# FFN pair products: t2 made by a third accumulating transfer, the splits in another order, and product 1 with 512 columns

## Chip, core and metric

The kernel runs on one core of a Trainium2 chip, with 512 tokens, in fp32. The time is device microseconds of one execution. A core has a matrix engine (PE, with its weight loads as PEld), a vector engine (DVE), an activation engine (ACT), GpSimd (POOL) and a queue engine that mostly issues transfers (SP, "sync"). Each engine runs its own instructions in order.

## The reference, cut to what matters

One layer of a hybrid encoder: a SwiGLU feed-forward half step (FFN1), a token mixer of two attention branches with gates, and a second feed-forward half step (FFN2). The model width is 1024 and D_FF is 2816.

```python
def _swiglu(x, w_gate, w_up, w_down):
    return (jax.nn.silu(x @ w_gate) * (x @ w_up)) @ w_down
...
        f = _swiglu(_rmsnorm(x, ffn1_pre_g[l]), ffn1_w_gate[l], ffn1_w_up[l], ffn1_w_down[l])
        x = x + 0.5 * _rmsnorm(f, ffn1_post_g[l])
...
        f = _swiglu(_rmsnorm(x, ffn2_pre_g[l]), ffn2_w_gate[l], ffn2_w_up[l], ffn2_w_down[l])
        x = x + 0.5 * _rmsnorm(f, ffn2_post_g[l])
```

The change touches the products `x @ w_gate` and `x @ w_up` of both feed-forward steps.

## The kernel before, in words

**Products in parts.** Every fp32 operand is split in a high and a low part (`split`: ACT rounds a copy at L113, DVE subtracts it at L114), and a product is taken in three passes, high by high, high by low and low by high (`mm3`, L204 to L206). The 2816 features of gate and up are 22 blocks of 128. Two blocks of each are done plainly. The other 20 are *pairs* j = 0 to 19: gate block j and up block j are the two rows of a 2 by 2 block product (the other two divisions are the two halves of the 1024 inputs and the two halves, 256 each, of the tokens).

**Seven products.** A 2 by 2 product by the Strassen-Winograd scheme needs seven products of 512 inputs by 128 features by 256 tokens instead of eight, and sums of weight blocks ahead of them. For a pair, with `gate` and `up` as 128 by 1024 blocks whose halves are [:512] and [512:], the weight blocks by the number of their product are

- 1 and 2: gate[:512] and gate[512:], the two halves of one 512 KB tile `raw`, of which a ring holds two
- 3: up[512:], named w11
- 5: t1 = up[:512] + gate[:512], loaded by SP and then summed by an accumulating transfer that POOL issues (L404)
- 7: t3 = up[:512] + up[512:], in the same way (L405)
- 6: t2 = t1 + w11, a DVE addition (L410, in `sums_of`)
- 4: t4 = t2 + gate[512:], a DVE addition (L415)

`load_blocks` issues the transfers of a pair two pairs ahead; `ready(j + 1, i)` prepares (sums and splits) block i of the next pair while PE works on pair j, in the program's order 1, 5, 2, 6, 3, 7, 4. A ring of 38 tiles of 256 KB (`up`) holds the blocks and results, a ring of 12 the split weights (`w`).

**Wide and narrow products.** A narrow product is 12 matmuls of 256 columns. A wide one (`WIDE`, L461 and L464) puts the high and the low part of the tokens side by side: four matmuls of 512 columns, weight-high by [high | low], fill a whole PSUM bank with two halves, and four of 256 columns add weight-low by high to the lower half. The two halves are summed by whoever reads the bank. Before the change product 1 is always narrow; products 5, 6, 3, 7 and 4 are wide in the pairs of `state["wide"]` (4 to 17 in FFN1, all in FFN2), and product 2 up to pair 16. For pairs 0 to 3 products 1 and 2 are made earlier (`EARLY`).

**Order on PE.** In iteration j PE runs 1(j); the 512-column halves of 7(j-1) and 5(j), then their 256-column halves; then the 512-column halves of 2(j), 6(j), 4(j-1) and 3(j), then theirs. This order is pinned to the program's. Bank q holds 1(j), then 6(j), 7(j), 4(j) are added in it; p holds 5(j), then 3(j); r holds 2(j).

**Readers of the banks.** ACT copies q after product 1 into g (L495). DVE subtracts q after 7(j-1) from a copy of p (L506, with L507 adding the halves), adds r to g (L521, two additions for the two halves), and after 6 and 3 makes the up results (L529, L536, L537). DVE and ACT keep the order that the framework's scheduler gives them when the kernel is built; SP is in the program's order in FFN1. There SP's queue also carries up to seven small transfers of the attention bias for each pair (L1247).

Of the kernel before, what the change touches and what calls it, by code (L numbers as in the profile page):

```python
# [16 lines left out]
ALU = mybir.AluOpType  # L17
# [7 lines left out]
NF = 2816 // P  # L25
# [1 line left out]
EPS = 1e-6  # L27
NEG = -1.0e30
NUNIT = 38
WIDE = (5, 2, 6, 3, 7, 4)  # L30
PIECE = 1024
NPIECE = 6
SPREAD = 4
# [2 lines left out]
STD = 2  # L36
EARLY = 4
# [9 lines left out]
def block_kernel(ctx, tc, x, gains, weights, rpb_near, rpb_all, alibi0, alibi12, out):  # L47
    nc = tc.nc
# [12 lines left out]
    def unit(dt=F32, name="u"):  # L61
        return up.tile([P, 512], dt, tag="u", name=name)
# [57 lines left out]
    state = {"used": False, "next": 0, "take": 0, "stop": EARLY + 2 * STD, "ahead": lambda: None}  # L120
# [231 lines left out]
    def combined():  # L352
# [17 lines left out]
        for n, of in ((5, lambda i: (whole[0][i], whole[1][i], sub)), (6, lambda i: (v[5][i], a[0][i], sub)),  # L370
# [5 lines left out]
            for i in range(2):  # L376
                if n in WIDE:
                    t = twin("v").rearrange("p (k s t) -> p k s t", k=2, s=2)
# [7 lines left out]
        whole.clear()  # L386
        yield mv

    def load_blocks(n0, j):

        w11, t1, t3 = unit(name="w11"), unit(name="t1"), unit(name="t3")
        gate, up = (n0 + j, n0 + EARLY + 2 * STD + j) if j < EARLY else [n0 + 2 * STD + 2 * j + i for i in range(2)]
        nc.sync.dma_start(t1, weights[up][:, :512])
        nc.sync.dma_start(t3, weights[up][:, :512])
        raw = {3: w11, 5: t1, 7: t3}
        if j < EARLY:
            raw[4] = unit(name="t4")
            nc.sync.dma_start(raw[4], weights[gate][:, 512:])
        else:
            r = wp.tile([P, PIECE], F32, tag="raw", name="raw", bufs=2)  # L400
            nc.sync.dma_start(r, weights[gate])
            raw[1], raw[2] = r[:, :512], r[:, 512:]
        nc.sync.dma_start(w11, weights[up][:, 512:])
        nc.gpsimd.dma_start(t1, weights[gate][:, :512], accum_op=ALU.add)  # L404
        nc.gpsimd.dma_start(t3, weights[up][:, 512:], accum_op=ALU.add)  # L405
        return raw

    def sums_of(raw):
        raw[6] = unit(name="t2")
        nc.vector.tensor_tensor(raw[6], raw[5], raw[3], op=ALU.add)  # L410
        if 4 in raw:
            nc.vector.tensor_tensor(raw[4], raw[6], raw[4], op=ALU.add)
        else:
            raw[4] = unit(name="t4")
            nc.vector.tensor_tensor(raw[4], raw[6], raw[2], op=ALU.add)  # L415

    def split_block(raw):
        w = wp.tile([P, PIECE], F32R, tag="w", name="w")
        split(w[:, :512], w[:, 512:], raw)
        return w  # L420

    def seven(use, mv, n_pairs, n0, behind, far, lead, raws, early, put, pin):

        blocks = {}
        o = {}

        def get(j):
            if j < n_pairs and j > 2:
                raws[j] = load_blocks(n0, j)
            if j >= n_pairs - 1:
                behind(far)

        def ready(j, i):
            if j < n_pairs:
                if j and loads:
                    loads.popleft()()  # L440
                if i == 1:
                    sums_of(raws[j])
                if j >= EARLY or i not in (1, 2):
                    blocks[j, i] = split_block(raws[j].pop(i))
            else:
                behind(lead)

        def product(j, i, key, start):
            if start:
                o[key, j] = bank(key)  # L450
            w = blocks.pop((j, i))
            high = [w[:, k * P:(k + 1) * P] for k in range(4)]
            low = [w[:, 512 + k * P:512 + (k + 1) * P] for k in range(4)]
            acc = o[key, j][:, :256]
            if i not in WIDE or j not in state["wide"] or (key in "qr" and j < EARLY) or (i == 2 and j > NF - STD - 4):
                for k in range(4):
                    mm3(acc, high[k], low[k], *mv[i][k][:2], start and k == 0, k == 3, skip_group_check=True)
                return
            for k in range(4):
                to = shaped(o[key, j], mv[i][k][2])  # L460
                nc.tensor.matmul(to, high[k], mv[i][k][2], start=start and k == 0, stop=False, skip_group_check=True)  # L461
            yield
            for k in range(4):
                nc.tensor.matmul(acc, low[k], mv[i][k][0], start=False, stop=k == 3, skip_group_check=True)  # L464

        def run(*products):
            products = [product(*p) for p in products]
            for _ in range(2):
                for p in products:
                    next(p, None)  # L470

        def full(j):
            return j in state["wide"] and j >= EARLY

        res = {}
        get(0)
        get(1)
        blocks[0, 5] = split_block(raws[0][5])
        ready(0, 1)
        raws[0].pop(5)  # L480
        for i in (6, 3, 7, 4):
            ready(0, i)
            if i == 3:
                put()
        begin = mark()
        for j in range(n_pairs + 1):
            now, was = j < n_pairs, j > 0
            get(j + 2)
            if now:
                if j < EARLY:  # L490
                    o["q", j], g = early[j]
                else:
                    run((j, 1, "q", True))
                    g = unit(name="g")
                    nc.scalar.copy(g[:, :256], o["q", j][:, :256])  # L495
                u = unit(name="up")
                res[j] = g, u, unit(name="p5") if j in state["wide"] else u[:, 256:]
            ready(j + 1, 1)
            if pin and j == 0:
                pool.append((pin, mark(), (mybir.EngineType.DVE,)))  # L500
            run(*[(j - 1, 7, "q", False)] * was, *[(j, 5, "p", True)] * now)
            if was:
                g0, u0, s0 = res.pop(j - 1)
                q0 = o["q", j - 1]
                if full(j - 1):
                    nc.vector.tensor_tensor(s0, s0, q0, op=ALU.subtract)  # L506
                    nc.vector.tensor_tensor(u0[:, 256:], s0[:, :256], s0[:, 256:], op=ALU.add)  # L507
                else:
                    nc.vector.tensor_tensor(u0[:, 256:], s0[:, :256], q0[:, :256], op=ALU.subtract)
                if j - 1 in state["wide"] and not full(j - 1):  # L510
                    nc.vector.tensor_tensor(u0[:, 256:], u0[:, 256:], s0[:, 256:], op=ALU.add)
            ready(j + 1, 5)
            if now:
                p = o["p", j]
                nc.scalar.copy(res[j][2], p if j in state["wide"] else p[:, :256])
            ready(j + 1, 2)
            two = now and j >= EARLY
            run(*[(j, 2, "r", True)] * two, *[(j, 6, "q", False)] * now, *[(j - 1, 4, "q", False)] * was, *[(j, 3, "p", False)] * now)
            if two:
                for part in range(1 + (full(j) and j <= NF - STD - 4)):  # L520
                    nc.vector.tensor_tensor(g[:, :256], g[:, :256], o["r", j][:, part * 256:part * 256 + 256], op=ALU.add)  # L521
            ready(j + 1, 6)
            if now:
                nc.scalar.copy(u if full(j) else u[:, :256], o["q", j] if full(j) else o["q", j][:, :256])
            ready(j + 1, 3)
            if was:
                if full(j - 1):
                    nc.scalar.copy(g0[:, 256:], q0[:, 256:])
                    nc.vector.tensor_tensor(g0[:, 256:], q0[:, :256], g0[:, 256:], op=ALU.add)  # L529
                    use(j - 1, g0, u0, g0[:, 256:])  # L530
                else:
                    use(j - 1, g0, u0, q0[:, :256])
            ready(j + 1, 7)
            if now:
                if full(j):
                    nc.vector.tensor_tensor(u, p, u, op=ALU.subtract)  # L536
                    nc.vector.tensor_tensor(u[:, :256], u[:, :256], u[:, 256:], op=ALU.add)  # L537
                else:
                    nc.vector.tensor_tensor(u[:, :256], p[:, :256], u[:, :256], op=ALU.subtract)
                if j in state["wide"] and not full(j):  # L540
                    nc.vector.tensor_tensor(u[:, :256], p[:, 256:], u[:, :256], op=ALU.add)
            ready(j + 1, 4)
        pool.append((begin, mark(), (mybir.EngineType.PE,)))
# [1025 lines left out]
    raws = []  # L1569
# [9 lines left out]
    for n in range(2, 4):  # L1579
        raw = wp.tile([P, PIECE], F32, tag="raw", name="raw", bufs=2)  # L1580
# [233 lines left out]
```

## Time and profile before

| | us |
|---|---|
| median of 3 runs (1069.28 to 1071.21) | 1069.45 |
| the profiled execution | 1069.0 |
| its span, first to last instruction | 1067.1 |
| PE busy | 1059.0 |
| DVE busy | 871.7 |
| ACT busy | 650.7 |
| POOL busy | 196.8 |

A row of a timeline is start, duration, engine, line of the kernel, operation, output and inputs, and in brackets the idle time before it and what ended that. Names stand without their buffer numbers there, so a block made in a ring shows as `w` or `t`. "DMA to landing" is the time from the issue of a transfer to its last byte as seen by who waits for it. PE's matmuls overlap, so the distance from start to start tells what one costs, and the duration when its result is there.

### The profile page before, as it was taken

The numbers are of one execution on the slowest core, as the hardware profiler recorded it, in microseconds if no ns is written. First come the engines' busy times: TensorE is split into PE (matmuls) and PEld (weight loads), VectorE is DVE, ScalarE is ACT, GpSimd is POOL, SyncE is SP. The second block draws the span as 40 slices with busy tenths as digits, with TensorE's granted clock in tenths as the row PEclk, the third lists the DMA queues.
The fourth block names the chain that finished last, engine by engine and source line by source line (L and its number), as shares of the span: only waits on it lengthen the run. The fifth ranks groups of instructions, "written<-read, shape, count | busy, mean of one in ns | idle before, by whom it ended". The sixth has DMA issues, their size and how long they took to land.

```text
span 1067.1 us, 17185 instructions
## 1 busy us (share of the span) xinstructions
PE 1059.0 (99%) x5955; PEld 922.5 (86%) x5955; DVE 871.7 (82%) x1694; ACT 650.7 (61%) x1346; POOL 196.8 (18%) x261
## 2 busy tenths in 40 slices
PE   9999999999999999999999999999999999999997
PEld 7899988998888988888988888889899899988886
DVE  7999999989987566676876643877998999989985
ACT  7656656566674665567756641366655566667671
POOL 4112111024334000001100001043301111124201
PEclk9999999999999999999999999999999999999999
DMA  9988988679993554322232239585937777879942
GB/s 335 201 217 234 236 206 202 194 187 264 248 311 115 157 168 150 119 71 69 81 106 79 79 115 304 151 199 191 285 93 191 175 189 198 219 205 246 219 180 80
DMA packets 98026, 193.95 MB, mean 182 GB/s; under 512 B 24337, under 2 KB 26897, under 8 KB 97938
## 3 DMA queue, kind: packets, MB, share of 16 engines
q1 hardware_dynamic: 69760, 138.37, 38.7%
q0 software_dynamic: 25488, 54.01, 27.9%
q8 instruction: 47, 0.77, 0.3%
q10 hardware_dynamic: 2690, 0.46, 0.2%
q14 instruction: 41, 0.34, 0.1%
HBM read 185.68 MB, written 9.68 MB: 183 GB/s over the span
## 4 chain that ended last, share of the span: by engine, by line
PE 99%; DMA 0%; DVE 0%; ACT 0%; SPq 0%; issue 0%; DVEq 0%; ACTq 0%
PE ps L204 11%; PE ps L206 11%; PE ps L205 11%; PE q L461 8%; PE q L206 7%; PE q L205 7%; PE q L204 7%; PE p L461 6%; PE q L464 4%; PE p L464 3%; PE r L461 2%; PE c L206 2%; PE c L205 2%; PE c L204 2%; PE r L205 1%; PE r L206 1%
## 5 line engine op out<-in xcount | busy, mean ns | idle before, releaser
L114 DVE TENSOR_TENSOR w<-raw,w 128x512 fp32r<-128x512 f32 (+1 forms) x142 | 130.8, 925 | 72.5 <-ACT w L113 69.2
L113 ACT CAST w<-t 128x512 fp32r<-128x512 f32 x160 | 98.1, 622 | 113.9 <-DVE t L410 62.9
L113 ACT CAST w<-raw 128x512 fp32r<-128x512 f32 (+1 forms) x142 | 114.0, 809 | 78.8 <-PE ps L205 30.8
L204 PE MATMUL ps<-hn,w 128*128 128x512 f32 (+1 forms) x360 | 136.6, 379 | 0.0
L206 PE MATMUL ps<-hn,w 128*128 128x512 f32 (+1 forms) x360 | 134.6, 374 | 0.0
L205 PE MATMUL ps<-hn,w 128*128 128x512 f32 (+1 forms) x360 | 134.4, 373 | 0.0
L114 DVE TENSOR_TENSOR w<-t,w 128x512 fp32r<-128x512 f32 x160 | 108.2, 684 | 0.2
L404 POOL DMA_DIRECT2D t<-in_weights_dram x40 | 35.0, 875 | 286.5 <-DVE w L114 78.1
L206 PEld LDWEIGHTS ps<-hn,w 128*128 128x128 f32 x360 | 67.8, 188 | 12.7 <-DVE w L114 0.7
L204 PEld LDWEIGHTS ps<-hn,w 128*128 128x128 f32 x360 | 67.9, 189 | 11.4
L205 PEld LDWEIGHTS ps<-hn,w 128*128 128x128 f32 x360 | 67.9, 189 | 10.9
L461 PE MATMUL p<-v,w 128*128 128x512 f32 x272 | 73.1, 390 | 0.0
L113 ACT CAST w<-room 128x1024 fp32r<-128x1024 f32 x49 | 51.5, 1053 | 30.1 <-PE q L206 9.3
L114 DVE TENSOR_TENSOR w<-room,w 128x1024 fp32r<-128x1024 f32 x49 | 59.6, 1220 | 7.1 <-ACT w L113 3.1
L461 PE MATMUL q<-v,w 128*128 128x512 f32 x240 | 65.1, 393 | 0.0
L461 PEld LDWEIGHTS p<-v,w 128*128 128x128 f32 x272 | 50.4, 188 | 10.2
L731 POOL DMA_DIRECT2D rows<-in_weights_dram x36 | 35.3, 1199 | 93.3 <-DVE w L114 62.8
L461 PEld LDWEIGHTS q<-v,w 128*128 128x128 f32 x240 | 43.0, 189 | 7.5
L113 ACT CAST w<-rows 128x512 fp32r<-128x512 f32 x62 | 36.0, 618 | 20.2 <-PE q L206 7.2
L206 PE MATMUL q<-hn,w 128*128 128x256 f32 x168 | 47.6, 283 | 0.0
L205 PE MATMUL q<-hn,w 128*128 128x256 f32 x168 | 47.5, 283 | 0.0
L204 PE MATMUL q<-hn,w 128*128 128x256 f32 x168 | 47.5, 283 | 0.0
(335 smaller groups left out, 3015.0 us busy)
## 6 DMA issues: line engine op xcount, KB each, us to landing
raw<-in_weights_dram SPq DMA_DIRECT2D x94, 512.0 KB
t<-in_weights_dram SPq DMA_DIRECT2D x88, 256.0 KB
t<-in_weights_dram POOLq DMA_DIRECT2D x80, 256.0 KB, 5.9
room<-in_weights_dram SPq DMA_DIRECT2D x37, 512.0 KB
room<-in_weights_dram POOLq DMA_DIRECT2D x29, 512.0 KB, 11.7
w<-in_weights_dram SPq DMA_DIRECT2D x40, 256.0 KB
rows<-in_weights_dram POOLq DMA_DIRECT2D x36, 256.0 KB, 7.8
w<-in_weights_dram POOLq DMA_DIRECT2D x32, 256.0 KB, 8.0
```

The lines of the kernel that those rows point to most:

```text
L113: nc.scalar.copy(hi, src)
L114: nc.vector.tensor_tensor(lo, src, hi.bitcast(F32), op=ALU.subtract)
L204: nc.tensor.matmul(o, sh, mh, start=start, stop=False, **kw)
L205: nc.tensor.matmul(o, sh, ml, start=False, stop=False, **kw)
L206: nc.tensor.matmul(o, sl, mh, start=False, stop=stop, **kw)
L404: nc.gpsimd.dma_start(t1, weights[gate][:, :512], accum_op=ALU.add)
L461: nc.tensor.matmul(to, high[k], mv[i][k][2], start=start and k == 0, stop=False, skip_group_check=True)
L464: nc.tensor.matmul(acc, low[k], mv[i][k][0], start=False, stop=k == 3, skip_group_check=True)
L731: nc.gpsimd.dma_start(u, block(*add, d)[:, cs], accum_op=ALU.add)
```

## The change

Two things are changed, for pairs 4 to 16 of each FFN. *Product 1 becomes wide*: eight matmuls instead of twelve (5955 matmuls become 5851 in the kernel). ACT still copies the lower half of q into g, and a new DVE addition (L511 of the changed kernel) adds the upper half to g; 6(j), which writes into the same bank, has to wait until that has read it. *t2 is no longer summed by DVE*: the blocks are split in the order 5, 1, 2, 3, 6, 7, 4; when t1 has been split (5), POOL issues a third accumulating transfer that adds up[512:] from the memory onto t1's own tile (L458), which makes t2 there; 6 is split from it, and t4 is summed at the end, just before it is split (L454). With that, `raw` is held until the sum of t4. DVE has one addition of 512 columns less and one of 256 columns more in a pair; the memory is read for 256 KB more in a pair.

```diff
-WIDE = (5, 2, 6, 3, 7, 4)
+WIDE = (1, 5, 2, 6, 3, 7, 4)
...
+    def up_block(n0, j):
+        return weights[n0 + 2 * STD + 2 * j + 1]
+
...
-                if i == 1:
-                    sums_of(raws[j])
-                if j >= EARLY or i not in (1, 2):
-                    blocks[j, i] = split_block(raws[j].pop(i))
+                raw = raws[j]
+                if not EARLY <= j <= NF - STD - 4:
+                    if i == 1:
+                        sums_of(raw)
+                    if j >= EARLY or i not in (1, 2):
+                        blocks[j, i] = split_block(raw.pop(i))
+                    return
+                i = {1: 5, 5: 1, 6: 3, 3: 6}.get(i, i)
+                if i == 4:
+                    raw[4] = unit(name="t4")
+                    nc.vector.tensor_tensor(raw[4], raw.pop(6), raw.pop(2), op=ALU.add)
+                blocks[j, i] = split_block(raw[i] if i in (2, 5, 6) else raw.pop(i))
+                if i == 5:
+                    raw[6] = raw.pop(5)
+                    nc.gpsimd.dma_start(raw[6], up_block(n0, j)[:, 512:], accum_op=ALU.add)
...
-            if i not in WIDE or j not in state["wide"] or (key in "qr" and j < EARLY) or (i == 2 and j > NF - STD - 4):
+            if i not in WIDE or j not in state["wide"] or (key in "qr" and j < EARLY) or (i in (1, 2) and j > NF - STD - 4):
...
+                    if full(j) and j <= NF - STD - 4:
+                        nc.vector.tensor_tensor(g[:, :256], g[:, :256], o["q", j][:, 256:], op=ALU.add)
```

The lines behind the first of these stand 3, then 14 to 16 further on in the changed kernel: L404, L405 are L407, L408 there; L506, L507 are L522, L523; L521 is L537; L529, L536, L537 are L545, L552, L553; L461 is L475.

On DVE, in iteration 10 of FFN1, these rows follow the subtraction of q after 7(9) (p5 is the copy of p of pair 9, g the gate result of pair 10, r and q banks). Before, with the sums and splits of blocks of pair 11:

```order
L506 TENSOR_TENSOR p5_1716<-p5_1716,q_1700 128x512
L410 TENSOR_TENSOR t2_1843<-t1_1691,w11_1690 128x512
L507 TENSOR_TENSOR up_1715<-p5_1716 128x256
L415 TENSOR_TENSOR t4_1845<-t2_1843,raw_1695 128x512
L114 TENSOR_TENSOR w_1914<-t2_1843,w_1914 128x512
L114 TENSOR_TENSOR w_1919<-w11_1690,w_1919 128x512
L114 TENSOR_TENSOR w_1929<-t3_1692,w_1929 128x512
L521 TENSOR_TENSOR g_1838<-g_1838,r_1878 128x256 x2
```

After, from the sum of t4 of pair 10 to the splits of t2 and t3 of pair 11:

```order
L454 TENSOR_TENSOR t4_1785<-t1_1551,raw_1555 128x512
L522 TENSOR_TENSOR p5_1692<-p5_1692,q_1679 128x512
L114 TENSOR_TENSOR w_1787<-t4_1785,w_1787 128x512
L523 TENSOR_TENSOR up_1691<-p5_1692 128x256
L114 TENSOR_TENSOR w_1815<-t1_1670,w_1815 128x512
L114 TENSOR_TENSOR w_1839<-raw_1674,w_1839 128x512
L114 TENSOR_TENSOR w_1844<-raw_1674,w_1844 128x512
L114 TENSOR_TENSOR w_1883<-w11_1669,w_1883 128x512
L511 TENSOR_TENSOR g_1809<-g_1809,q_1800 128x256
L114 TENSOR_TENSOR w_1888<-t1_1670,w_1888 128x512
L114 TENSOR_TENSOR w_1898<-t3_1671,w_1898 128x512
```

The subtraction of p5 stands ahead of the splits of t4, t1, both halves of raw and w11, and the new addition of q's upper half to g behind all of them. So it is in pairs 6, 8, 10, 12, 14 and 16 of FFN1; in the others it stands directly ahead of the subtraction.

On DVE in FFN2, around the end of iteration 6 and the beginning of 7 (p5 of pair 6, g of pair 7). Before, from the split of t4 of pair 7 to that of t2 of pair 8:

```order
L114 TENSOR_TENSOR w_9294<-t4_9210,w_9294 128x512
L536 TENSOR_TENSOR up_9206<-p_9219,up_9206 128x512
L114 TENSOR_TENSOR w_9328<-raw_9186,w_9328 128x512
L529 TENSOR_TENSOR g_9086<-q_9073,g_9086 128x256
L537 TENSOR_TENSOR up_9206<-up_9206 128x256
L114 TENSOR_TENSOR w_9350<-t1_9182,w_9350 128x512
L410 TENSOR_TENSOR t2_9324<-t1_9182,w11_9181 128x512
L114 TENSOR_TENSOR w_9354<-raw_9186,w_9354 128x512
L638 TENSOR_TENSOR h_9171<-up_9088,g_9086 128x256
L506 TENSOR_TENSOR p5_9207<-p5_9207,q_9191 128x512
L415 TENSOR_TENSOR t4_9326<-t2_9324,raw_9186 128x512
L114 TENSOR_TENSOR w_9392<-t2_9324,w_9392 128x512
```

After, from the sum of t4 of pair 7, which reads t1's tile with the third transfer's sum in it, to the new addition in pair 7:

```order
L454 TENSOR_TENSOR t4_9227<-t1_9007,raw_9011 128x512
L552 TENSOR_TENSOR up_9142<-p_9152,up_9142 128x512
L545 TENSOR_TENSOR g_9025<-q_9016,g_9025 128x256
L114 TENSOR_TENSOR w_9213<-t1_9007,w_9213 128x512
L553 TENSOR_TENSOR up_9142<-up_9142 128x256
L114 TENSOR_TENSOR w_9222<-t3_9008,w_9222 128x512
L114 TENSOR_TENSOR w_9229<-t4_9227,w_9229 128x512
L114 TENSOR_TENSOR w_9256<-t1_9121,w_9256 128x512
L114 TENSOR_TENSOR w_9279<-raw_9125,w_9279 128x512
L114 TENSOR_TENSOR w_9283<-raw_9125,w_9283 128x512
L522 TENSOR_TENSOR p5_9143<-p5_9143,q_9130 128x512
L511 TENSOR_TENSOR g_9251<-g_9251,q_9242 128x256
```

There the new addition of pair 7 stands behind the sum of t4, the splits of t2, t3 and t4 of pair 7, and those of t1 and raw of pair 8. So it is in every second pair (7, 9, 11, 13 and 15).

On POOL, in FFN1 (t1 and t3 are the tiles of pairs 9 to 11). Before:

```order
L404 DMA t1_1443<-in_weights_dram 128x512
L405 DMA t3_1444<-in_weights_dram 128x512
L404 DMA t1_1568<-in_weights_dram 128x512
L405 DMA t3_1569<-in_weights_dram 128x512
L404 DMA t1_1691<-in_weights_dram 128x512
L405 DMA t3_1692<-in_weights_dram 128x512
```

After:

```order
L407 DMA t1_1551<-in_weights_dram 128x512
L408 DMA t3_1552<-in_weights_dram 128x512
L458 DMA t1_1430<-in_weights_dram 128x512
L407 DMA t1_1670<-in_weights_dram 128x512
L408 DMA t3_1671<-in_weights_dram 128x512
L458 DMA t1_1551<-in_weights_dram 128x512
```

The third transfer of a pair (L458, into its t1 tile) stands behind the first two of the pair after it: that of pair 9 (t1_1430) behind t1_1551 and t3_1552, and that of pair 10 (t1_1551) behind t1_1670 and t3_1671.

## Prediction

> **What bounds the kernel now.** I read the page first (busy time, slices), then the waits of TensorE, then the two stretches that the change touches, by windows, and last the timelines of one pair on each engine. The page's head:
>
> ```profile
> span 1067.1 us, 17185 instructions
> PE 1059.0 (99%) x5955; PEld 922.5 (86%) x5955; DVE 871.7 (82%) x1694; ACT 650.7 (61%) x1346; POOL 196.8 (18%) x261
> PEclk9999999999999999999999999999999999999999
> q0 software_dynamic: 25488, 54.01, 27.9%
> t<-in_weights_dram POOLq DMA_DIRECT2D x80, 256.0 KB, 5.9
> ```
>
> TensorE (PE) is busy for 99% of the span at full clock. All the waits of PE that the trace has are two, at the start:
>
> ```profile
> PE warm L1591 <- DVE idle L1555: 1.2, 1, 1.2
> PE ps L326 <- DVE u L1620: 0.3, 1, 0.3
> ```
>
> So the kernel takes as long as PE's instructions take. The windows of the pair stages, FFN1 and then FFN2 (columns: PE, PEld, DVE, ACT, POOL, clock, DMA share, GB/s):
>
> ```profile
> 71.90:199.40 127.50, 127.50 (x791) 115.02 (x789) 118.06 (x231) 77.41 (x166) 24.70 (x28) 1.00 0.87 218
> 790.00:918.00 128.00, 128.00 (x800) 115.77 (x800) 118.12 (x234) 76.66 (x164) 21.80 (x26) 1.00 0.71 183
> ```
>
> PE has no gap there, VectorE (DVE) is busy for 118.06 of 127.50 us, 93%. A microsecond that PE loses there is lost to the end; a microsecond that DVE saves is worth nothing while PE never waits for it. One pair of FFN1 on PE, from product 1 (its first and last matmul of twelve) to the next product 1:
>
> ```profile
> 120.88 0.28 PE L204 MATMUL q<-hn,w 128*128 128x256 f32 x1
> ...
> 122.20 0.28 PE L206 MATMUL q<-hn,w 128*128 128x256 f32 x1
> 122.32 1.09 PE L461 MATMUL q<-v,w 128*128 128x512 f32 x4
> 123.25 1.07 PE L461 MATMUL p<-v,w 128*128 128x512 f32 x4
> 124.16 0.64 PE L464 MATMUL q<-v,w 128*128 128x256 f32 x4
> 124.63 0.64 PE L464 MATMUL p<-v,w 128*128 128x256 f32 x4
> 125.11 1.09 PE L461 MATMUL r<-hn,w 128*128 128x512 f32 x4
> 126.04 1.07 PE L461 MATMUL q<-v,w 128*128 128x512 f32 x4
> ...
> 128.76 0.64 PE L464 MATMUL r<-hn,w 128*128 128x256 f32 x4
> ...
> 130.68 0.28 PE L204 MATMUL q<-hn,w 128*128 128x256 f32 x1
> ```
>
> The period is 130.68 - 120.88 = 9.80 us. Call the start of product 1 T. Before the change the second half of 7(j-1) ends at T + 3.92 (124.16 + 0.64), 6(j), which adds into the bank that product 1 opened, starts at T + 5.16, and the last matmul of 2(j), which the subtraction of r reads, ends at T + 8.52.
>
> **Fewer matmuls (a gain).** Product 1 now takes 122.32 - 120.88 = 1.44 us. Wide it is four of 512 columns (123.25 - 122.32 = 0.93) and four of 256 (124.63 - 124.16 = 0.47), 1.40 in all. The gain is 0.04 us in each of 13 pairs of each FFN, 26 x 0.045 = 1.2 us taken a little generously; everything above moves to T + 3.88 and T + 5.12, the period to 9.76.
>
> **The new DVE addition and where it stands (the largest loss).** PE's 6(j) must not write into bank q before the addition L511 has read its upper half, so L511 has to end by T + 5.12. What stands ahead of it on DVE decides, since DVE works in order. DVE rows of FFN1 before the change:
>
> ```profile
> 134.79 0.68 DVE L506 TENSOR_TENSOR p<-p,q 128x512 f32<-128x512 f32 x1
> 135.39 0.68 DVE L410 TENSOR_TENSOR t<-t,w 128x512 f32<-128x512 f32 x1
> 135.99 0.42 DVE L507 TENSOR_TENSOR up<-p 128x256 f32<-128x256 f32 x1
> 136.32 0.68 DVE L415 TENSOR_TENSOR t<-t,raw 128x512 f32<-128x512 f32 x1
> 136.93 0.68 DVE L114 TENSOR_TENSOR w<-t,w 128x512 fp32r<-128x512 f32 x1
> ```
>
> From start to start an operation on 512 columns takes 0.60 us and one on 256 columns 0.33 to 0.34 (0.42 to its end). In the changed order L511 stands, in pairs 6, 8, ..., 16 of FFN1, behind L522 (the p5 subtraction, L506 before), which reads what 7(j-1) wrote and so can't start before T + 3.88. Between the two lie a split of t4, L523 and the splits of t1, raw, raw and w11. That is L522 0.60, five splits 3.00, L523 0.34, L511 0.42: 4.36 us, so L511 ends at T + 8.24 at the earliest and PE stands still for 8.24 - 5.12 = 3.12 us. No DMA is in this sum and no slack can help: it begins at a result of PE. Six such pairs: **+18.7 us**. In the other pairs of FFN1 L511 stands just ahead of L522 and is done in time unless DVE is late.
>
> **The third transfer (a wait of DVE).** t2 was a DVE addition (0.60 us); now split5 (t1) must end, POOL issues the transfer, it lands after L, ACT casts the block and only then can DVE split 6, and t4's sum L454 wants the same landing. No row has this transfer; the nearest are the accumulating ones that exist, "DMA to landing" min/median/max, for t1 and t3 in FFN1, then for t1 and t3 in FFN2, and ACT's cast:
>
> ```profile
> DMA to landing us min/median/max: 4.1/5.0/6.0
> DMA to landing us min/median/max: 5.9/6.6/8.2
> DMA to landing us min/median/max: 3.6/3.9/4.1
> DMA to landing us min/median/max: 4.9/7.0/7.6
> 116.56 0.62 ACT L113 CAST w<-t 128x512 fp32r<-128x512 f32 x1 [2.79 <-DVE t L410]
> ```
>
> t3's is issued right behind t1's and lands later. The new one stands behind both in POOL's queue, but waits for DVE's split5, so it is often apart from them: I take L = 5.5 in FFN1, where the DMA share is 0.87, and 5 in FFN2 (0.71), between t1's and t3's, and 4 and 7 as the ends. The Trainium skill ("DMA: Bandwidth & Descriptors", "Anatomy of one DMA — SWDGE (gpsimd) path") puts a GpSimd transfer at 2.0 us and its bytes by 436e3, by estimate 2.6 us for 256 KB; the trace disagrees with its 3.6 to 8.2, and by that rule the whole sum would be that of the second rival below, 1090.
>
> FFN1, over two pairs: in a late pair split5 ends at T + 6.1 (3.88 + 3 x 0.60 + 0.34 and 0.09 to its end), so DVE can split 6 at 6.1 + L + 0.62 = T + 12.2. From there to the next pair's L511 stand split6, split7, L537, t4's sum, L537, L552, L545, split4, L553, split5, raw, raw and L654: eight long and five short, 6.5 us, and L511's 0.42, so T + 19.1. PE wants it at 8.24 + (9.76 - 5.12) + 5.12 = T + 18.0: 1.1 late. The same chain once more (split5 ends at T + 17.2, split6 at T + 23.3, then four long and seven short up to L522, 4.8 us) comes to L522 of the next late pair at T + 28.1, where its operand is there at T + 12.88 + 9.76 + 1.1 + 3.88 = T + 27.6: 0.5 late. Together 3.1 + 1.1 + 0.5 = 4.7 us in two pairs, 6 x 4.7 = **+28 us** for FFN1, the 18.7 among them. With L up to 4.4 nothing is added (18.7); with 7 it is 3.1 + 2.6 + 2.0 = 7.7, or 46 us.
>
> FFN2: in one of two pairs the two L537 end at T + 9.1 (8.48 and two short ones), and behind them t4's sum needs split5's end (T + 5.75) + L = T + 10.75. From its start to the end of the next pair's L511 stand nine long operations (the sum, L552, splits of 6, 7, 4, t1, raw and raw, L522), two short ones and 0.42, 6.5 us: T + 17.25, where PE wants it at 9.76 + 5.12 = T + 14.9. It is late by 2.4 us in five pairs (7, 9, ..., 15): **+12 us**. That is L - 2.6, and no less than 0.8, the value up to L = 3.4; with 4 it is 7 us in all, with 7 it is 22.
>
> **Queues.** The new transfer stands in POOL's queue behind t1's and t3's of the pair after its own, which wait for loads on SP, and these stand behind a load of raw that waits until t4's sum of two pairs earlier has released the tile:
>
> ```profile
> 137.07 0.33 SPq L401 DMA_DIRECT2D raw<-in_weights_dram  x1
> 137.51 0.35 SPq L403 DMA_DIRECT2D w<-in_weights_dram  x1
> 137.91 5.02 SPq L1247 DMA_DIRECT2D bias_d<-bias_r  x7
> 142.98 0.45 SPq L393 DMA_DIRECT2D t<-in_weights_dram  x1
> 147.38 0.87 POOL L404 DMA_DIRECT2D t<-in_weights_dram  x1 [7.45 <-DVE w L114]
> 148.01 1.14 POOL L405 DMA_DIRECT2D t<-in_weights_dram  x1
> ```
>
> With t4's sum over at 137.00 (136.32 + 0.68), t1's transfer went out at 147.38, 10.4 us later, 5 of them bias transfers. Add 1.8 for the two issues, L 5.5, the cast 0.6 and three DVE operations up to the next t4's sum (1.6): 19.9 us in a loop of two pairs, which take 19.5 + 4.7 = 24.2. It isn't the bound; with L = 8 and loads that come 3 us later it is 25.4, and does what the third rival says. The extra bytes cost 27.9% x 1067.1 / 54.01 = 5.5 us per MB of the 16 engines, 1.44 us for 0.262 MB in 9.8 us: to a share of 0.87 that is 0.15, over 1 but for the longer period. This speaks for the higher L.
>
> ACT gets no new operation, PE none. DVE's total falls by 0.60 - 0.34 a pair, worth nothing.
>
> **Sum.** -1.2 + 28 + 12 = +38.8 us on the profiled run's own 1069.0 (span 1067.1 and 1.9 around it), which is 0.4 below the median 1069.45 of the runs shown: 1107.8, **1108**.
>
> **The rivals.**
> *The other side: DVE is relieved and nothing waits.* If L511 were done by T + 5.12 everywhere and L458 had landed when DVE comes to split 6 (raw, raw, L654, L511, L522, w11 and L523 stand between, 3.4 us in the better pairs, so L under 2.8), only PE's 1.2 us would be left: 1067.8. That is within 0.2% (2.1 us, about what a measurement of this kernel can tell). For it: DVE is idle for 9.4 and 9.9 us of the two stages. Against it: the chain of 4.36 us from PE's own result. Chance 0.05.
> *Only the place of L511 counts* (L of 3.4 or less): 18.7 + 5 x 0.8 - 1.2 = +21.5, 1090. For it: t1's transfer in FFN2 lands after 3.6 to 4.1; against it FFN1's 4.1 to 8.2. Chance 0.2.
> *The queues and DMA bound FFN1 and L grows to 7*: 46 + 22 - 1.2 = +67, 1136. For it: the share of 0.87. Against it: a longer period relieves the DMA again. Chance 0.18.
> *The clock falls in the new gaps.* If after a gap PE ran at half clock for as long as the gap had lasted, 3.1 us would cost another 1.6 in six places and 2.4 another 1.2 in five, 15 us: 1122. The trace has a clock of 9 tenths or more in all slices, and no gap of over 1.2 us to show it. The Trainium skill ("TensorE: Matmul & The Clock Gate", "Part 1: The HAM clock gate") lets the clock fall to half when PE was idle in a window of some 3.4 us. Chance 0.08.
> *The change doesn't do what it says* can be excluded for the matmuls (5955 become 5851); it is not a case.
>
> **How the numbers follow.** The forecast (L 4.5 to 6 in both stages) has 0.49, from 19 + 9.5 - 1.2 (1096) to 34 + 17 - 1.2 (1119), at 1108. The range takes in the second rival (1090, less 2 for its bounds) and part of the third: 1088 to 1133; the rest of it, the other side and a clock far down lie outside. Slower 0.95; within 0.2% 0.03; faster 0.02, which would need more than the 1.2 us that PE has to win.
>
> **What would show it.** PE's waits in the profile after: `q` of product 6 (L475) for DVE `g` (L511), 3.1 us or more in six pairs of FFN1 and 1.4 to 3.4 in five of FFN2; PE busy shorter by about 1.2 us; L458's landing 4 to 7 us; DVE waiting for ACT's cast of t1 or for L458. Wrong would be: no wait at L511 (then the DVE order didn't hold what it shows), gaps elsewhere on PE (weights that come late), or FFN1 losing less than 18.7.

## The result, and the profile after

The changed kernel takes **1143.8 us** (median of 4 runs, 1143.17 to 1144.79) against 1069.37 before: 1.0697 times as long, 95% interval 1.0683 to 1.0710. The sign was forecast, the size was not: the loss is 74 us, 39 were forecast, and the time lies above the range. The heads of its page:

```profile
span 1143.0 us, 17044 instructions
PE 1086.4 (95%) x5851; PEld 930.5 (81%) x5851; DVE 865.3 (76%) x1694; ACT 651.5 (57%) x1346; POOL 217.5 (19%) x287
PEclk9998888989999999999999999999999999999999
q0 software_dynamic: 29232, 60.83, 30.0%
PE 66%; DVE 12%; DMA 11%; issue 5%; ACT 4%; POOL 1%; SPq 0%; DVEq 0%; ACTq 0%; POOLq 0%
```

The last line is the chain that ended last, by engine. It was 99% PE; now a third of it runs over DVE, a DMA and ACT. PE's span grew by 75.9 us, and the first lines split that: PE's idle time went from 8.1 (1067.1 - 1059.0) to 56.6 us (1143.0 - 1086.4), 48.5 more, and PE's busy time grew by 27.4 us although it has 104 matmuls less. The first part is PE's new waits; the second is matmuls that took longer, most of it by a lower clock:

```profile
PE q L475 <- DVE g L511: 42.8, 17, 4.6
PE q L475 <- ACT up L540: 3.2, 4, 1.4
PE p L475 <- ACT p L531: 2.8, 4, 0.8
```

```profile
core 0: 1143.0 us, clock 0.976
```

The windows from the start of product 2 of pair 4 to that of pair 16 (twelve periods) in FFN1 and FFN2, with the columns of the prediction:

```profile
75.90:238.00 162.10, 133.85 (x679) 112.98 (x678) 105.85 (x215) 72.48 (x155) 33.54 (x38) 0.89 0.76 176
851.20:991.70 140.50, 125.38 (x677) 105.87 (x677) 103.09 (x211) 70.31 (x150) 30.50 (x35) 0.96 0.75 174
```

Before, the same twelve periods take 117.66 us (76.05 to 193.71) and 117.67 (800.01 to 917.68). FFN1 loses 44.4 us there and 6.9 more up to FFN2 (from 606.3 to 613.2; the wait ahead of product 6 of pair 16 is among that), FFN2 22.9 and 1.9 behind it. DVE is busy for only 65% and 73% of these windows, and yet it is DVE's order that makes the time. One cycle of two pairs in FFN1 shows how. PE, with its long gap in a late pair (pair 8):

```profile
131.27 1.09 PE L475 MATMUL r<-hn,w 128*128 128x512 f32 x4
136.94 2.07 PE L475 MATMUL q<-v,w 128*128 128x512 f32 x4 [4.57 <-DVE g L511]
138.81 1.91 PE L475 MATMUL q<-hn,w 128*128 128x512 f32 x4
...
149.28 1.07 PE L475 MATMUL q<-v,w 128*128 128x512 f32 x4
```

DVE in the same cycle (the splits of t1, x1 at 134.06 and 146.29, and the splits of t2 and t3, x2, that wait for ACT's cast):

```profile
132.30 0.68 DVE L522 TENSOR_TENSOR p<-p,q 128x512 f32<-128x512 f32 x1
...
134.06 0.68 DVE L114 TENSOR_TENSOR w<-t,w 128x512 fp32r<-128x512 f32 x1
...
136.47 0.41 DVE L511 TENSOR_TENSOR g<-g,q 128x256 f32<-128x256 f32 x1
141.04 1.29 DVE L114 TENSOR_TENSOR w<-t,w 128x512 fp32r<-128x512 f32 x2 [4.16 <-ACT w L113]
142.91 0.42 DVE L537 TENSOR_TENSOR g<-g,r 128x256 f32<-128x256 f32 x1 [0.58 <-PE r L478]
...
146.29 0.68 DVE L114 TENSOR_TENSOR w<-t,w 128x512 fp32r<-128x512 f32 x1
...
154.21 1.29 DVE L114 TENSOR_TENSOR w<-t,w 128x512 fp32r<-128x512 f32 x2 [3.83 <-ACT w L113]
```

And the third transfer's issues on POOL, each released by DVE's split, with ACT's casts that its landing releases:

```profile
135.04 0.87 POOL L458 DMA_DIRECT2D t<-in_weights_dram  x1 [4.84 <-DVE w L114]
147.27 0.87 POOL L458 DMA_DIRECT2D t<-in_weights_dram  x1 [2.37 <-DVE w L114]
```

```profile
140.39 1.14 ACT L113 CAST w<-t 128x512 fp32r<-128x512 f32 x2 [4.47 <-DMA t<-in_weights_dram]
153.56 1.14 ACT L113 CAST w<-t 128x512 fp32r<-128x512 f32 x2 [4.42 <-DMA t<-in_weights_dram]
```

Read in order: split of t1 ends (134.74), transfer out (135.04), landed (140.39), split of t2 (141.04), DVE's other work, split of t1 of the next pair (to 146.97), transfer (147.27), landed (153.56), split of t2 (154.21), and so on. That is a loop that goes from DVE over POOL, a DMA and ACT back to DVE, twice in two pairs. It takes about 27 us, where PE has 19.5 us to do.

### The profile page after: what moved, and what is told of

It is laid out like the page before. It is cut to its first block, busy times and chain, and to the rows that moved or that the text cites. A ratio compares the mean times of both kernels' runs of the same rounds, so it can differ in the third digit from the quotient of the medians.

```text
span 1143.0 us, 17044 instructions
## 1 busy us (share of the span) xinstructions
PE 1086.4 (95%) x5851; PEld 930.5 (81%) x5851; DVE 865.3 (76%) x1694; ACT 651.5 (57%) x1346; POOL 217.5 (19%) x287
## 4 chain that ended last, share of the span: by engine, by line
PE 66%; DVE 12%; DMA 11%; issue 5%; ACT 4%; POOL 1%; SPq 0%; DVEq 0%; ACTq 0%; POOLq 0%
DMA t<-in_weights_dram 10%; PE ps L204 9%; PE ps L205 9%; PE ps L206 9%; DVE w L114 5%; PE q L475 5%; PE q L206 4%; PE q L204 4%; PE q L205 4%; PE p L475 2%; PE c L206 2%; ACT w L113 2%; PE c L204 2%; PE c L205 2%; PE q L478 2%
## 5 line engine op out<-in xcount | busy, mean ns | idle before, releaser
L113 ACT CAST w<-t 128x512 fp32r<-128x512 f32 x160 | 92.5, 619 | 146.4 <-DMA t<-in_weights_dram 102.4
L114 DVE TENSOR_TENSOR w<-t,w 128x512 fp32r<-128x512 f32 x160 | 105.3, 685 | 80.2 <-ACT w L113 79.7
L113 ACT CAST w<-raw 128x512 fp32r<-128x512 f32 (+1 forms) x142 | 111.4, 807 | 75.2 <-PE ps L205 28.8
L475 PE MATMUL q<-v,w 128*128 128x512 f32 x240 | 73.3, 430 | 46.2 <-DVE g L511 42.8
L475 PEld LDWEIGHTS q<-v,w 128*128 128x128 f32 x240 | 43.9, 199 | 61.6 <-DVE g L511 50.2
L475 PE MATMUL p<-v,w 128*128 128x512 f32 x272 | 80.2, 420 | 2.8 <-ACT p L531 2.8
L407 POOL DMA_DIRECT2D t<-in_weights_dram x40 | 35.3, 883 | 195.4 <-DMA t<-in_weights_dram 109.3
L475 PEld LDWEIGHTS p<-v,w 128*128 128x128 f32 x272 | 55.2, 208 | 16.7 <-ACT p L531 4.6
L475 PE MATMUL q<-hn,w 128*128 128x512 f32 x224 | 68.1, 430 | 0.0
L475 PEld LDWEIGHTS q<-hn,w 128*128 128x128 f32 x224 | 45.4, 211 | 9.0
L458 POOL DMA_DIRECT2D t<-in_weights_dram x26 | 23.2, 890 | 146.2 <-DVE w L114 146.2
```

The costliest lines, as they stand in the source:

```text
L113: nc.scalar.copy(hi, src)
L114: nc.vector.tensor_tensor(lo, src, hi.bitcast(F32), op=ALU.subtract)
L458: nc.gpsimd.dma_start(raw[6], up_block(n0, j)[:, 512:], accum_op=ALU.add)
```

## The experiments

All times are medians beside the kernel before on the same chip (1069.1 to 1069.5). The table gives, beside the time, the twelve periods of FFN1 and of FFN2, from the starts of product 2 of pairs 4 and 16 on PE; these two columns are of each kernel's one profiled execution, whose time lay off the median in two rows (1131.0 for the change with ACT copying all of q, 1100.8 for t2 by DVE).

| kernel | us | ratio, 95% | FFN1 | FFN2 |
|---|---|---|---|---|
| before | 1069.4 | | 117.7 | 117.7 |
| the change | 1143.8 | 1.0697 (1.0683 to 1.0710) | 162.1 | 140.6 |
| product 1 wide alone | 1079.6 | 1.0098 (1.0083 to 1.0113) | 121.9 | 121.5 |
| the same, ACT copies all of q | 1069.1 | 0.9996 (0.9987 to 1.0005) | 117.3 | 117.3 |
| third transfer alone | 1132.6 | 1.0589 (1.0572 to 1.0607) | 155.4 | 138.3 |
| the change, ACT copies all of q | 1137.3 | 1.0643 (1.0626 to 1.0661) | 155.4 | 135.6 |
| the change, PE's gaps filled | 1138.4 | 1.0645 (1.0629 to 1.0661) | 161.1 | 137.9 |
| the change, t2 by DVE | 1105.1 | 1.0342 (1.0311 to 1.0372) | 144.4 | 119.2 |
| the same, ACT copies all of q | 1078.1 | 1.0083 (1.0069 to 1.0097) | 124.3 | 117.6 |
| t2 in its own tile, ACT copies all of q | 1104.5 | 1.0328 (1.0314 to 1.0342) | 142.6 | 126.7 |
| third transfer of half the columns | 1127.3 | 1.0537 (1.0519 to 1.0554) | 154.2 | 133.6 |
| the change, PE's product 6 later | 1141.2 | 1.0668 (1.0639 to 1.0696) | 156.5 | 137.5 |

**Product 1 wide alone.** The splits and t2 are put back:

```diff
-                raw = raws[j]
-                if not EARLY <= j <= NF - STD - 4:
...
+                if i == 1:
+                    sums_of(raws[j])
+                if j >= EARLY or i not in (1, 2):
+                    blocks[j, i] = split_block(raws[j].pop(i))
```

> Product 1 wide alone; t2 and the order of the splits as before the change. Theory (the loss is L511 queued on DVE behind the p5 subtraction and four splits, plus DVE waiting for the third transfer, plus a half clock after gaps of 4 us): without the third transfer L511 stands at most behind the p5 subtraction and one addition (it ends at T + 5.5 where PE wants it at T + 5.12), so gaps of about 0.4 us in every second pair, no fall of the clock, PE 1.2 us less: 1069 to 1073 us. Rival (the wide product with its addition is the loss by itself, wherever it stands): 1090 us or more, with gaps of 3 us.

1079.6 us, between the two expectations. The waits are as small as the theory had them, twelve of 0.48 us (the addition is L500 there):

```profile
PE q L464 <- DVE g L500: 5.8, 12, 0.5
```

```profile
116.16 1.09 PE L464 MATMUL r<-hn,w 128*128 128x512 f32 x4
117.73 1.20 PE L464 MATMUL q<-v,w 128*128 128x512 f32 x4 [0.48 <-DVE g L500]
118.77 1.07 PE L464 MATMUL q<-hn,w 128*128 128x512 f32 x4
```

But a period with one is longer by 0.78 us: from 116.16 to 118.77 are 2.61 us where two groups of four take 1.83 without a wait (0.92 and 0.91). The break in the stream of matmuls costs some 0.3 us more than the wait that is shown, 12 x 0.78 = 9.4 us in all. Most of the 10.5 us is in that.

**The same, with ACT copying all 512 columns of q**, so that the bank is free after one ACT copy and the addition reads only SBUF:

```diff
-                    nc.scalar.copy(g[:, :256], o["q", j][:, :256])
-                    if full(j) and j <= NF - STD - 4:
-                        nc.vector.tensor_tensor(g[:, :256], g[:, :256], o["q", j][:, 256:], op=ALU.add)
+                    two_halves = full(j) and j <= NF - STD - 4
+                    nc.scalar.copy(g if two_halves else g[:, :256], o["q", j] if two_halves else o["q", j][:, :256])
+                    if two_halves:
+                        nc.vector.tensor_tensor(g[:, :256], g[:, :256], g[:, 256:], op=ALU.add)
```

> Product 1 wide alone with ACT copying all 512 columns of q; t2 and the splits as before the change. Theory: the 12 waits of 0.48 us and their breaks (10 us) go, PE has 1.2 us less to do: 1067 to 1069 us, perhaps just faster than before. Rival (the extra columns on ACT or the addition on DVE cost as much): 1072 us or more.

1069.1 us, no difference that this measurement tells from the kernel before. Every wait of PE in the pair stages is gone, and the periods are 9.77 instead of 9.80 us: the wide product does save 0.033 us a pair, 0.8 us in the 24 periods. Of that the whole kernel shows nothing; in this profile PE lost 1.2 us between the two stages, where it waited 0.8 for DVE.

**The third transfer alone**, product 1 narrow and no addition L511:

```diff
-WIDE = (1, 5, 2, 6, 3, 7, 4)
+WIDE = (5, 2, 6, 3, 7, 4)
...
-                    if full(j) and j <= NF - STD - 4:
-                        nc.vector.tensor_tensor(g[:, :256], g[:, :256], o["q", j][:, 256:], op=ALU.add)
```

> The third transfer and the new order of the splits alone; product 1 narrow as before, so no L511 and no wait of PE for it. Theory: DVE still waits 2 to 4 us for the landing in each pair, and its loop of two pairs takes 16.8 us of work and 2.5 to 7 us of waits against 19.6 us of PE, so PE is held by late DVE results: 1085 to 1105 us, more gaps and smaller ones, little loss of clock. Rival (only L511's place counts, the transfer is hidden): 1069 to 1072 us.

1132.6 us: more than the theory had, and the rival falls. 63 of the 74 us are here without any L511. PE now waits for ACT:

```profile
PE q L475 <- ACT g L509: 22.5, 8, 3.1
PE q L475 <- ACT up L538: 11.1, 13, 1.8
PE p L475 <- ACT p L529: 8.0, 6, 1.5
PE q L475 <- DVE p L520: 4.4, 7, 1.1
```

The copy of q (L509) stands on ACT behind casts that wait for DVE's sum t4, and on DVE that sum comes 4.3 us behind the split that waits for the landing (123.68 and 128.02 in this pair):

```profile
128.80 1.14 ACT L113 CAST w<-t 128x512 fp32r<-128x512 f32 x2 [1.44 <-DVE t L454]
...
131.40 0.36 ACT L509 COPY g<-q 128x256 f32<-128x256 f32 x1
```

```profile
131.81 1.26 PE L475 MATMUL q<-v,w 128*128 128x512 f32 x4 [3.11 <-ACT g L509]
```

The wait that L511 showed on PE was only the last link; take it away and the next one stands there.

**The change with ACT copying all of q**, the edit shown above in the changed kernel.

> The whole change, but ACT copies all 512 columns of q into g and the addition reads only g, so that PE's product 6 waits for the ACT copy and not for DVE. Theory: the 3.1 us that L511's place costs in every second pair of FFN1 and the fall of the clock go, DVE's loop with the landing remains: 1085 to 1110 us, as the transfer alone. Rival (L511's wait is all of it): 1068 to 1071 us. Second rival (the addition is not the cause, DMA and queues are): 1135 us or more.

1137.3 us, only 6.5 less. The rival that L511's wait is all of it is wrong, and so is the 1085 to 1110 of the theory, which had the loop too short. The time lies in the range of the second rival (1135 or more). That is right in that the addition is not the main cause; what it means by DMA and queues is tested below, by the third transfer in a tile of its own.

**The change with PE's gaps filled.** Matmuls with weights of zero ahead of product 6:

```diff
+            if key == "r":
+                first = 0 not in state["wide"]
+                for _ in range(28 * (j in range(6, 17, 2)) if first else 16 * (j in range(7, 16, 2))):
+                    nc.tensor.matmul(acc[:64], zeros, ident.bitcast(BF16), start=False, stop=False, skip_group_check=True)
             yield
```

> The whole change, and in pairs 6, 8, ..., 16 of FFN1 28 matmuls of 256 columns with weights of zero (pairs 7, 9, ..., 15 of FFN2: 16) ahead of product 6, where PE stands still for 4.5 and 2.2 us; they add zero to bank r. Theory of the clock: PE busy for about 3 us of each gap keeps its clock, so the 29 us by which the other matmuls became longer mostly go: 1115 to 1125 us although PE has 2 us more to do in each place. Rival (the matmuls are longer for another reason, such as DMA traffic or the wait's release): 1140 to 1150 us.

The clock came back, to 0.995, and the group behind the gap takes 1.19 instead of 2.07 us:

```profile
136.66 1.19 PE L477 MATMUL q<-v,w 128*128 128x512 f32 x4 [1.40 <-DVE g L517]
...
162.39 1.19 PE L477 MATMUL q<-v,w 128*128 128x512 f32 x4 [1.39 <-DVE g L517]
```

The time did not: 1138.4, 5.4 us less. My expectation of 1115 to 1125 was wrong. The half clock is real and follows from the gap, but most of PE's slow matmuls run beside DVE's wait for the landing, and the loop still takes 25.7 us from one of these gaps to the next.

**The change with t2 summed by DVE** on t1's tile, all else (order of the splits, L511) as changed:

```diff
-                    nc.gpsimd.dma_start(raw[6], up_block(n0, j)[:, 512:], accum_op=ALU.add)
+                    nc.vector.tensor_tensor(raw[6], raw[6], raw[3], op=ALU.add)
```

> The whole change, but t2 is made by a DVE addition onto t1's tile in place of the third transfer; the splits stay in the new order, and L511 stays behind the p5 subtraction and five splits or sums in every second pair of FFN1. Theory (two limits: DVE's loop of two pairs with two landings in it, 26.9 us in FFN1 and 24 in FFN2 against 19.6 of PE, and apart from it L511's place): the loop is gone in both stages, FFN2's period goes back to 9.8 us, and in FFN1 gaps of 3.7 us are left in six pairs with a break of PE's stream of 0.4 and some half clock: 1093 to 1106 us. Rival (the landing is all of it): 1068 to 1075. Rival (L511's place is all of it): 1120 or more.

1105.1 us, in the range of the theory. FFN2 is back at 9.9 us a pair; in FFN1 the gaps of pairs 6 to 14 are 3.65 us each, where 3.7 was worked out. They also show the clock by itself, three of them:

```profile
102.44 2.07 PE L475 MATMUL q<-v,w 128*128 128x512 f32 x4 [3.65 <-DVE g L511]
128.63 2.07 PE L475 MATMUL q<-v,w 128*128 128x512 f32 x4 [3.65 <-DVE g L511]
153.76 1.19 PE L475 MATMUL q<-v,w 128*128 128x512 f32 x4 [3.65 <-DVE g L511]
```

The same gap of 3.65 us halves the clock twice and then not. Where it does, two pairs take 26.2 us (128.63 - 102.44) and 25.1 (153.76 - 128.63), where it doesn't, 23.9 (the next groups start at 177.61 and 201.53): the fall costs 2.3 us the first time and 1.2 the second, when the half clock lasted 3.4 us in place of 6.8.

**The same, with ACT copying all of q.**

> As the run before, and ACT copies all 512 columns of q, so that PE waits for that copy and not for the DVE addition. Theory: both limits are gone, 1067 to 1075 us. Rival (the new order of the splits costs by itself, with raw released late): 1080 us or more.

1078.1 us, just above the theory's 1067 to 1075. FFN2 is free of it; in FFN1 six waits of 1 us are left, again for a copy that stands on ACT behind casts:

```profile
PE q L475 <- ACT g L510: 5.9, 6, 1.1
```

The kernel with the wide product and the same copy, but t2 and the order of the splits as before, took 1069.1 on the same chip. So the new order, with raw held longer, costs 9.0 us by itself, without any third transfer; which of the two it is was not tried. That is just short of what the rival said (1080 or more).

**t2 in a tile of its own**, so that the third transfer does not wait for DVE's split of t1:

```diff
+        if EARLY <= j <= NF - STD - 4:
+            raw[6] = unit(name="t2")
+            nc.sync.dma_start(raw[6], weights[up][:, 512:])
+            nc.gpsimd.dma_start(raw[6], t1, accum_op=ALU.add)
...
-                    nc.gpsimd.dma_start(raw[6], up_block(n0, j)[:, 512:], accum_op=ALU.add)
```

> The whole change with ACT copying 512 columns, and t2 made in a tile of its own: SP loads up[512:] there and the third accumulating transfer adds t1's tile from SBUF right after t1 and t3, without waiting for DVE's split of t1. The third transfer stays and the traffic grows by 256 KB more a pair; only the landing leaves DVE's loop. Theory of the loop: FFN2's period goes back to 9.8 to 10.3 us, FFN1 keeps at most what the transfers need, 10.8 us: 1068 to 1090 us. Rival (the bytes or POOL's queue are the limit, not where the wait stands): as with the copy by ACT alone or slower, 1130 us or more.

1104.5 us: 33 less than with the landing in the loop (1137.3, with the same copy by ACT), with 256 KB more to move for each pair. So neither the bytes nor POOL's queue set the time there, but I had expected still less. What PE still waits for is ACT: 20.9 us for the copy of q, and 4.6 in FFN1 for the copy of p, which there comes behind a cast that still waits for the landing. In FFN2, DVE no longer waits for a landing, but ACT's copy L511 (the copy of q in this kernel) comes behind six casts, and PE behind it:

```profile
865.93 1.14 ACT L113 CAST w<-t 128x512 fp32r<-128x512 f32 x2 [1.38 <-DVE t L458]
...
869.06 0.57 ACT L511 COPY g<-q 128x512 f32<-128x512 f32 x1
```

```profile
869.68 1.19 PE L476 MATMUL q<-v,w 128*128 128x512 f32 x4 [1.59 <-ACT g L511]
```

**A third transfer of half the columns.**

```diff
-                    nc.gpsimd.dma_start(raw[6], up_block(n0, j)[:, 512:], accum_op=ALU.add)
+                    nc.gpsimd.dma_start(raw[6][:, :256], up_block(n0, j)[:, 512:768], accum_op=ALU.add)
```

> The whole change, but the third transfer adds only the first 256 of the 512 columns (the other half of t2 stays t1, so products 6 and 4 are computed from another block). Theory (two landings stand in DVE's loop of two pairs): if half the bytes land 1.5 us earlier in FFN1 and 0.8 earlier in FFN2, the period of two pairs falls by twice that, from 27 to 24 us in FFN1, where L511's place takes over at 23.9, and from 24 to 22.4 in FFN2: 1108 to 1125 us, and the fall of the periods is twice the fall of the landing time. Rival (L511's place bounds already): 1138 to 1145.

This kernel leaves the last 256 columns of up[512:] out of t2. 1127.3 us, just above the range; the rival falls. The median landing fell by 1.2 us in FFN1 (6.2 to 5.0) and by 0.1 in FFN2 (4.6 to 4.5), but the medians hide what counts in the loop, which is the sum. In FFN1 the twelve landings in the window came to 69.9 us and now come to 61.4; the twelve periods fell by 7.9 us, nearly as much. In FFN2 every second landing is a long one, 5.3 to 7.9 us, and now 4.4 to 5.5: the eleven in the window fell from 61.0 to 50.8 us, and the periods by 7.0. So the periods follow the landings, as the theory has it. In FFN1 DVE's waits for the cast in the cycle above shrank from about 4 to 2.7 and 1.8 us, and the cycle from 27 to 25.3. There the other limit comes in too: a gap of 3 to 4 us for L511's place, 2.7 us of half clock, and 19.5 of work:

```profile
133.05 2.08 PE L475 MATMUL q<-v,w 128*128 128x512 f32 x4 [4.02 <-DVE g L511]
158.30 1.78 PE L475 MATMUL q<-v,w 128*128 128x512 f32 x4 [3.05 <-DVE g L511]
```

The scheduler also changed DVE's order in this kernel in a few rows (the split of t1 stands ahead of its neighbour). What part of the gain is that order stays open.

**PE's product 6 later**, behind 4(j-1) and 3(j):

```diff
-            run(*[(j, 2, "r", True)] * two, *[(j, 6, "q", False)] * now, *[(j - 1, 4, "q", False)] * was, *[(j, 3, "p", False)] * now)
+            run(*[(j, 2, "r", True)] * two, *[(j - 1, 4, "q", False)] * was, *[(j, 3, "p", False)] * now, *[(j, 6, "q", False)] * now)
```

> The whole change, but PE does 4(j-1) and 3(j) ahead of 6(j), so that it needs L511 1.8 us later. Theory (DVE's loop with the landings is the limit, and PE's gaps only move): 1128 to 1142 us. Rival (PE's wait for L511 is the loss as such): 17 waits shorter by up to 1.8 us and no half clock, 1100 to 1120 us.

1141.2 us, as the loop would have it. (The window of FFN1 is shorter only because it begins 5.4 us later, at 81.25; it ends at 237.8 as in the changed kernel.) The waits for L511 fell from 42.8 to 1.9 us, and others took their place:

```profile
PE q L475 <- ACT up L540: 25.0, 21, 2.3
PE q L475 <- DVE p L522: 16.9, 18, 1.6
```

## Why the prediction was wrong

**Right: the sign, and L511's place.** The 3.12 us that DVE's order costs at least, worked out from rows of the profile before, stand in the changed kernel. In pair 14, where DVE came in time to L522, the gap is 3.10 us:

```profile
216.69 1.56 PE L475 MATMUL q<-v,w 128*128 128x512 f32 x4 [3.10 <-DVE g L511]
```

In the other five pairs that were named it is 4.4 to 4.6, since DVE came late. (Pair 4, not named, has one of 3.0.) Where t2 is made by DVE the same sum with one addition more gives 3.7, measured 3.65.

**Right in size: the gain of PE.** 0.045 us a pair was said, 0.033 measured.

**Wrong: the size of the loop with the landing.** The step that failed is "FFN1, over two pairs", which came to 4.7 us by letting DVE split 6 at split5's end + L + 0.62. It made DVE's loop 24.2 us, the same as PE's; it is 26.9. Two sizes were short. From the end of split5 to the start of split6 pass 6.3 and 7.2 us (134.74 to 141.04, 146.97 to 154.21) and not 6.12. The hand-offs, 0.3 us to POOL's issue and 0.65 from the landing over the cast to DVE, make 0.95 and not 0.62, and the landings, 5.35 and 6.29, are 0.6 longer together than twice my 5.5: 1.3 us in a cycle, half of it each. And DVE's work between was 5.9 and 7.4 us, 13.3 in all, where I had counted 12.0, partly since it waits for PE inside it, 0.58 of it for r. 1.3 and 1.3 us short, 2.7 in each of six cycles, 16 us. FFN1 lost 51.3 us in all (44.4 and 6.9), 23 more than the 28 forecast; the rest of that is about one cycle more, since the gap came in seven pairs, 4 among them, and not in six.

**Wrong: FFN2 as one late sum.** I gave it 2.4 us in five pairs, from t4's sum to L511. The same loop runs there, with shorter landings. One cycle, by the issues of the third transfer:

```profile
908.60 0.86 POOL L458 DMA_DIRECT2D t<-in_weights_dram  x1 [4.92 <-DVE w L114]
...
922.21 0.86 POOL L458 DMA_DIRECT2D t<-in_weights_dram  x1 [8.42 <-DVE w L114]
...
930.98 0.86 POOL L458 DMA_DIRECT2D t<-in_weights_dram  x1 [4.56 <-DVE w L114]
```

That is 22.4 us here, and 23.4 on the mean of the six cycles (140.5 / 6), where 19.5 + 2.4 = 21.9 were forecast; 25 us were lost in place of 12. The step that failed there is that only t4's sum was taken to wait for the landing, without the way over the cast and the splits to the next issue.

**The clock: a rival that came true, and is not a term.** I put the fall of the clock in a case by itself at 0.08, where it excluded the forecast. It came along with it: the gaps are 4.4 to 4.6 us, and about 3 us after the last matmul (132.36) the clock falls to half, by windows of one microsecond:

```profile
134.00:135.00 1.00, 0.00 (x0) 0.00 (x0) 1.00 (x3) 1.00 (x3) 0.00 (x0) 1.00 0.76 172
135.00:136.00 1.00, 0.00 (x0) 0.00 (x0) 1.00 (x3) 0.91 (x3) 0.87 (x1) 0.70 0.93 338
136.00:137.00 1.00, 0.06 (x1) 0.07 (x1) 0.88 (x2) 0.00 (x0) 0.00 (x0) 0.50 0.98 276
```

PE's busy time, which I had 1.2 us shorter, grew by 27.4 us, some by the slower clock and some by the breaks in its stream, but with the gaps filled the kernel is only 5.4 us faster. Most of the 27 us runs beside the loop. Had I added the 15 us of that rival to the sum, the number would have been nearer and the reason wrong.

**The queues: nearest in number, not in mechanism.** The third rival's 1136 came from SP and POOL and from an L of 7. All of POOL's waits ahead of the third transfer end with DVE's split, and the landings' medians are 6.2 us in FFN1 and 4.6 in FFN2:

```profile
POOL t L458 <- DVE w L114: 52.0, 12, 9.0
```

```profile
DMA to landing us min/median/max: 4.7/6.2/7.4
DMA to landing us min/median/max: 4.1/4.6/7.9
```

Only once, in the first cycle of FFN1, did the transfers of the next pair hold it up in POOL's queue: DVE's split was over at 77.79, they went out at 79.16 and 79.84, and the third at 80.39, 2.6 us late. A kernel without the bias transfers on SP was not tried.

**Overlooked: ACT.** "ACT gets no new operation" was true and not enough. ACT works in order too, and its copies out of PE's banks stand behind casts that now wait for a landing. There PE's waits stand when L511 is gone, and the transfer alone still costs 63 us.

So the loss is the third transfer's place in a loop over DVE and ACT: by itself 63 us, with L511 74. L511's place by itself, with t2 by DVE, is 36, of which 27 go when ACT frees the bank. The costs do not add (63 and 36 are more than 74), since they run beside each other. No version that was run is faster than the kernel before.

## What to carry to other kernels

Where an engine that works in order has to start a transfer and later wait for it, add up the whole loop (work to the issue, hand-offs, landing, hand-offs, work to the next issue) and set it against the period of the engine that bounds, each hand-off counted; here DVE, 93% busy, had no room for a landing, although the transfer saved it an operation. Then look what else stands behind the wait in each queue that it reaches, above all reads that free a bank: moving one of them to another engine or a later place only shows the next. And costs that lie in one gap, such as a slower clock after a wait, are not summed until it is shown that nothing longer runs beside them.

## What the runs showed of the hardware

A wait that is shown as 0.48 us cost PE 0.78 by the starts of its groups: the group behind it starts 1.57 us after the one before (116.16 to 117.73), where it is 0.92 without a wait, and the next one 1.04 later in place of 0.91.

A gap of 3.65 us halved the granted clock in two cases and not in three, in the same run, for 2.3 and 1.2 us; with gaps of 1.4 us it stayed up. The record of the clock suggests why. In the changed kernel's FFN1 each stretch at half clock lasts 3.41 or 6.83 us, and the stretches start a multiple of 3.41 us apart (135.41, 162.71, 190.02 and 217.32 are 8 x 3.41 apart, 241.22 is 7 x 3.41 on). In the run with t2 by DVE the clock fell 2.0 and 3.1 us into the gap; carried on from there, the same steps of 3.41 us cut each of the other three gaps into two parts of at most 1.9 us. This part agrees with the Trainium skill ("TensorE: Matmul & The Clock Gate", "Part 1: The HAM clock gate"), by which the gate watches a window of about 3.4 us that runs freely and is not set off by the work. But PE need not be idle for a whole window: a gap of 2.24 us, in the change with ACT copying all of q, halved the clock 2.0 us after PE's last matmul. How the gaps lie in these steps may also be why the runs with t2 by DVE lie as far apart as 1100.8 and 1111.4, with mean clocks of 0.995 and 0.984.

An accumulating transfer of 256 KB landed after 4.1 to 7.9 us in the changed kernel, and one of 128 KB after 3.2 to 7.3. Half the bytes took 0.7 us off the mean in FFN1 (5.8 to 5.1) and 0.9 in FFN2 (5.5 to 4.6), so the bytes are not what takes most of the time. The estimate of 2.6 us that the prediction worked out by the Trainium skill ("DMA: Bandwidth & Descriptors", "Anatomy of one DMA — SWDGE (gpsimd) path") fits none of them.
